# Routing from un-normed rows, a float32 gather of rows without scale and shift, and a second spare slot for weights

## The chip, the cores and the metric

The kernel runs on one core of a Trainium2 chip. The metric is the device time of one execution in microseconds (us). The profile is of one execution of its own; its times count from the start of its span.

## What is computed

Two layers of a decoder trunk over 256 tokens of width 2048, in float32. Each layer is a mixer (a state-space mixer in layer 0, sparse attention in layer 1) and a mixture of 32 experts with two normalisations around it:

```python
h = _layer_norm(DN_ALPHA * h + mix, ln_mix_g[i], ln_mix_b[i])
ffn = _hier_moe(h, moe_w_group[i], moe_b_group[i], moe_w_expert[i], moe_b_expert[i],
                moe_w_gate[i], moe_w_up[i], moe_w_down[i])
h = _layer_norm(DN_ALPHA * h + ffn, ln_ffn_g[i], ln_ffn_b[i])
```

`_layer_norm` is `(x - mean) * rsqrt(var + eps) * g + b` by rows. In `_hier_moe` each token takes one of 4 groups by `softmax(t @ w_group + b_group)` and two of that group's 8 experts by `t @ w_expert + b_expert`; an expert is `silu(t @ w_gate) * (t @ w_up)` of width 256, scaled by its gate and multiplied by `w_down`.

## The kernel before

The tokens lie on 128 partitions in two halves; `acc` holds the residual rows in float32 (128 x 2 x 2048).

**Weights.** All large weights come in tiles of 128 x 4096 float32 (2.10 MB), in the fixed order of `plan`. `issue()` starts the next load, `take()` hands out the next loaded tile. The tiles are in a ring of six buffers (`RING`), and during a mixture in one more, the spare, from the pool `one`: which entries of the plan use it is in the set `spare`, every seventh. SP issues all of them, in program order, and waits at each for its buffer's last readers. A mixture takes 8 tiles of gate and up weights and 4 of down weights for each four experts ("a round"; eight rounds, `qd` 0 to 7).

**Around the router.** `out_proj` ends a mixer: PE multiplies, VectorE adds into `acc` (L800) and takes row statistics. The last entry of the mixer's plan is `gb`, which fills a ring buffer with `ln_mix_g` and `ln_mix_b`, each broadcast to all partitions. In `moe`, `layer_norm` computes the reciprocal root by three Newton steps; VectorE's `centre` (L869) does `(acc - mean) * g` and `shift` (L873) `acc * rs + b`, both in place, eight of each with 512 strided columns. PE transposes the centred rows (L222), ScalarE copies them out to `xT`, and PE multiplies them by the router's 36 weight columns (L1048) in float32; `bw` and `sbw` bring in what the shift adds to the logits. VectorE then makes logits, maxima and masks (L1092 to L1111), PE counts positions by triangular products, and VectorE writes one-hot matrices `ohr` (L1168) of 128 slots, 32 for each of four experts.

**Gather and experts.** The gather (L64 under `gather`) brings the rows of the 128 slots together: PE multiplies the normed rows by the one-hot matrix. Rows are split into a rounded part `xr` (ScalarE, L1065) and a remainder `xl` (VectorE, `st_xl`, L1069), both fp32r, so a chunk of 128 columns takes four fp32r products. A gather has four quarters of four chunks, each copied to `xs` by ScalarE (L1185). `gate_up` (L1279) multiplies by half of a round's gate, then up weights, and calls `issue()` twice after each pair of tiles is used. Then SiLU and gate (L1202, L1204), transposes, and `st_down` with `w_down`: its four blocks each read all four down tiles. `scatter` brings the results back to `acc`. After round 1's `gate_up`, `past_cap` is a branch on the largest expert's token count (its body does not run in this trace).

## Time and profile before

| | us |
|---|---|
| Median of 3 runs | 1735.82 (1734.8 to 1739.2) |
| The profiled execution, its own time | 1736.97 |
| Its span | 1735.3 |

| Engine | busy us | share of the span |
|---|---|---|
| PE | 1495.7 | 86% |
| VectorE (DVE) | 760.8 | 44% |
| ScalarE (ACT) | 493.3 | 28% |
| GpSimd (POOL) | 100.7 | 6% |

The page gives the busy share of the 16 DMA engines and the bytes moved in 40 equal slices, 43.4 us each. The chain of waits follows the work that ended last backwards. The timeline lists an engine's instructions in order of time, merged; for SP these are DMA issues, and a long duration there is the time from the first issue of the group to the last. A table by windows gives each engine's busy time, PE's granted clock and the DMA's share in a stretch.

### The profile page before, as it was taken

The numbers are of one execution on the slowest core, as the hardware profiler recorded it, in microseconds if no ns is written. First come the engines' busy times: TensorE is split into PE (matmuls) and PEld (weight loads), VectorE is DVE, ScalarE is ACT, GpSimd is POOL, SyncE is SP. The second block draws the span as 40 slices with busy tenths as digits, with TensorE's granted clock in tenths as the row PEclk, the third lists the DMA queues.
The fourth block names the chain that finished last, engine by engine and source line by source line (L and its number), as shares of the span: only waits on it lengthen the run. The fifth ranks groups of instructions, "written<-read, shape, count | busy, mean of one in ns | idle before, by whom it ended". The sixth has DMA issues, their size and how long they took to land. (4 is left out here: it accounts for less than half of the span.)

```text
span 1735.3 us, 28757 instructions
## 1 busy us (share of the span) xinstructions
PE 1495.7 (86%) x12119; PEld 1053.0 (61%) x12119; DVE 760.8 (44%) x1636; ACT 493.3 (28%) x1040; POOL 100.7 (6%) x225
## 2 busy tenths in 40 slices
PE   8999999999977788677788999999986887777687
PEld 7888888988633444343347998988744343433343
DVE  5788897666422012112207677966720121122015
ACT  3455564543311001000013455544410011000011
POOL 2111100001000000000001001400200000000000
PEclk8999999999896788899889999999987898988988
DMA  9565223855699999999996644345599999999994
GB/s 293 181 139 98 95 99 128 284 195 226 254 418 382 425 422 415 424 412 417 418 417 243 249 145 153 131 146 194 188 417 424 382 419 424 418 401 412 424 419 190
DMA packets 112938, 517.18 MB, mean 298 GB/s; under 512 B 8368, under 2 KB 41376, under 8 KB 71072
## 3 DMA queue, kind: packets, MB, share of 16 engines
q1 hardware_dynamic: 109664, 507.93, 73.8%
q0 software_dynamic: 3136, 7.31, 2.4%
q8 instruction: 99, 1.62, 0.4%
q14 instruction: 39, 0.32, 0.1%
HBM read 509.97 MB, written 5.24 MB: 297 GB/s over the span
## 5 line engine op out<-in xcount | busy, mean ns | idle before, releaser
L1279 PE MATMUL gu<-ring,xs 128*32 128x256 f32 x4096 | 317.9, 433 | 108.8 <-DMA ring<-in_moe_w_up_dram 84.0
L1279 PEld LDWEIGHTS gu<-ring,xs 128*32 128x32 f32 x4096 | 149.4, 123 | 265.2 <-DMA ring<-in_moe_w_up_dram 108.6
L64 PE MATMUL yd<-ring,hT 128*32 128x512 f32 x1024 | 187.9, 749 | 59.5 <-DMA ring<-in_moe_w_down_dram 58.4
L1204 DVE SCALAR_TENSOR_TENSOR hh<-gu,gsl,sg 128x256 f32<-128x256 f32 x16 | 7.7, 484 | 436.4 <-ACT sg L1202 436.4
L80 DVE TENSOR_TENSOR spl<-ring,spr 128x512 fp32r<-128x512 f32 x176 | 122.3, 696 | 78.1 <-ACT spr L79 75.1
L64 PE MATMUL mm<-ohr,xr 128*128 128x128 f32 x512 | 128.1, 293 | 32.7 <-DVE ohr L1168 19.1
L64 PEld LDWEIGHTS yd<-ring,hT 128*32 128x32 f32 x1024 | 37.4, 129 | 177.4 <-DMA ring<-in_moe_w_down_dram 88.7
L79 ACT ACTIVATE spr<-ring 128x512 fp32r<-128x512 f32 x176 | 110.7, 631 | 110.3 <-DVE spl L80 51.3
L80 DVE TENSOR_TENSOR yl<-yd,yr 128x512 fp32r<-128x512 f32 x64 | 44.3, 692 | 211.4 <-ACT yr L79 211.4
L64 PEld LDWEIGHTS mm<-ohr,xr 128*128 128x128 f32 x512 | 106.0, 207 | 45.3 <-issue 41.6
L64 PE MATMUL mm<-ohr,xl 128*128 128x128 f32 x512 | 127.3, 291 | 0.0
L1185 ACT ACTIVATE xs<-mm 128x512 f32<-128x512 f32 x64 | 38.2, 597 | 303.4 <-PE mm L64 303.4
L64 PE MATMUL u<-xT,ring 128*128 128x256 f32 x512 | 122.1, 393 | 2.2 <-DMA ring<-in_s_w_in_dram 1.4
L79 ACT ACTIVATE yr<-yd 128x512 fp32r<-128x512 f32 x64 | 38.3, 599 | 263.7 <-PE yd L64 263.7
L64 PEld LDWEIGHTS u<-xT,ring 128*128 128x128 f32 x512 | 97.6, 196 | 17.3 <-DMA ring<-in_s_w_in_dram 1.8
L64 PEld LDWEIGHTS mm<-ohr,xl 128*128 128x128 f32 x512 | 106.4, 208 | 0.1
L1202 ACT ACTIVATE sg<-gu 128x256 f32<-128x256 f32 x16 | 6.1, 384 | 264.9 <-PE gu L1279 264.9
L1250 DVE TENSOR_TENSOR acc<-acc,ps 128x512 f32<-128x512 f32 x112 | 72.6, 681 | 10.0 <-PE ps L64 10.0
L64 PE MATMUL ps<-yr,sc 128*128 128x512 f32 x128 | 58.6, 458 | 3.0 <-DVE acc L1250 2.0
L64 PEld LDWEIGHTS ps<-yr,sc 128*128 128x128 f32 x128 | 23.9, 187 | 60.1 <-issue 55.9
L1270 DVE TENSOR_SCALAR sc<-mm,slotp 128x256 fp32r<-128x256 f32 x16 | 7.7, 484 | 103.0 <-PE mm L64 103.0
L64 PE MATMUL mm<-spr,q 128*128 128x512 f32 x128 | 51.2, 400 | 0.0
(411 smaller groups left out, 2617.2 us busy)
## 6 DMA issues: line engine op xcount, KB each, us to landing
ring<-in_moe_w_gate_dram SPq DMA_DIRECT2D x128, 1024.0 KB, 15.9
ring<-in_moe_w_up_dram SPq DMA_DIRECT2D x128, 1024.0 KB, 19.6
ring<-in_moe_w_down_dram SPq DMA_DIRECT2D x56, 2048.0 KB, 24.8
ring<-in_s_w_glu_dram SPq DMA_DIRECT2D x8, 2048.0 KB, 9.5
ring<-in_s_w_out_dram SPq DMA_DIRECT2D x8, 2048.0 KB, 12.6
ring<-in_moe_w_down_dram SPq DMA_DIRECT2D x16, 1024.0 KB, 20.0
ring<-in_dsa_w_out_dram SPq DMA_DIRECT2D x8, 2048.0 KB, 8.1
ring<-in_s_w_in_dram SPq DMA_DIRECT2D x7, 2048.0 KB, 13.7
```

Source lines behind the costliest of these rows:

```text
L64: T.matmul(o, l, r, start=start, stop=stop)
L79: S.activation(dst[0], src, AF.Copy)
L80: V.tensor_tensor(dst[1], src, dst[0].bitcast(F32), op=OP.subtract)
L1185: S.activation(xs[:, 4 * q:4 * q + 4], p.rearrange("p (a b) -> p a b", a=4), AF.Copy)
L1202: S.activation(sg, gu[:, 0:FF], AF.Silu)
L1204: V.scalar_tensor_tensor(hh, gu[:, FF:2 * FF], g, sg, op0=OP.mult, op1=OP.mult)
L1250: V.tensor_tensor(acc[:, h, bs], acc[:, h, bs], ps, op=OP.add)
L1270: V.tensor_scalar(scs[qd], p[:, 0:L], slotp, None, op0=OP.is_equal)
L1279: T.matmul(gu[es, k * FF:(k + 1) * FF], xss[qd][:, 8 * half + c, es], w[e // 2][:, e % 2, c, :], start=half + c + k == 0, stop=half == 1 a ...
```

## The change

- **Router.** PE transposes the un-normed `acc` rows. `wr` holds router weights times `ln_mix_g` in 64 columns (32 expert, 8 empty, 4 group, 20 empty), made by GpSimd; mean and shift enter afterwards, by column sums `sw` (one PE product) and per-row scalars. The logits' product has the weights stationary and 256 tokens moving, in two halves of PE's columns (`o` 0 and 64) that `sel` adds up.
- **Gather.** `xz` is `(acc - mean) * rs` in float32 (`st_z`: half 0 on VectorE, half 1 on ScalarE); `xr`, `xl` are gone. A chunk takes two float32 products instead of four fp32r ones. Scale and shift come on leaving PSUM, by chunk, from `gTc`: ScalarE, and in the first two quarters of round 0 VectorE for every other chunk.
- **Residual.** `acc` is left un-normed until `residual`, 16 VectorE instructions during the second `gate_up` of round 0, with `ln_mix_g` and `ln_mix_b` loaded broadcast into buffers of `xs`, `yr`, `yl`. `gb` is out of the plan.
- **Weights.** The spare has two buffers (`bufs=2`), so there are eight; `moe` calls `issue()` twice at its start, and once less after the norm.

```diff
@@ issue, plan_s5 (and plan_dsa alike)
-            t = (spare_pool[0] if i in spare else ringp).tile([P, 4096], F32, name="ring", tag="ring")
+            t = (spare_pool[0].tile([P, 4096], F32, name="ring", tag="ring", bufs=2) if i in spare else
+                 ringp.tile([P, 4096], F32, name="ring", tag="ring"))
-        plan.append(gb("ln_mix_g", "ln_mix_b", 0))
@@ plan_moe
-        i = RING - 1
-        while i < len(todo):
-            spare.add(len(plan) + i)
-            last_spare[li] = len(plan) + i
-            i += RING + (i + RING < at_gb)
+        last_spare[li] = []
+        for i in (RING, RING + 1):
+            while i < len(todo):
+                spare.add(len(plan) + i)
+                k = i
+                i += RING + 2 - (i > at_gb)
+            last_spare[li].append(len(plan) + k)
@@ moe
-            issue()
+            issue(); issue()
...
+            for i, n in enumerate(("ln_mix_g", "ln_mix_b")):
+                nc.sync.dma_start(gTc[:, i], dram(A[n], li * D, [[KC, P], [1, KC]]))
...
+            G.memset(wr, 0.0)
+            for i, t in ((0, wr), (1, wb)):
+                if i:
+                    G.memset(wb, 0.0)
+                for w, a, n in ((wex, 0, 32), (wge, 40, 4)):
+                    G.tensor_tensor(t[:, :, a:a + n], w, gbT[:, i, :, None].to_broadcast([P, KC, n]), op=OP.mult)
...
+            for i, t in ((0, wr), (1, wb)):
+                G.tensor_tensor(sw[:, :, i], t[:, 0:8, 0:44], t[:, 8:16, 0:44], op=OP.add)
+            for n in (4, 2, 1):
+                G.tensor_tensor(sw[:, 0:n], sw[:, 0:n], sw[:, n:2 * n], op=OP.add)
...
-            centre, shift, rs = layer_norm(stt)
...
-            for q in range(4):
-                st_h(q)
-            issue()
+            def logits(b):
+                for c in range(4 * b, 4 * b + 4):
+                    o = 64 * (c % 2)
+                    T.matmul(plT[o:o + 64, 0:L], wr[:, c, :], xT[b][:, c % 4, :], start=c < 2, stop=c >= KC - 2,
+                             skip_group_check=True)
+            mv, ve = ln_moments(stt)
+            for b in range(NBLK):
+                for c in range(0, 4, 2):
+                    p = pmm.tile([P, 512], F32, name="mm")
+                    for c2 in range(2):
+                        for h in range(2):
+                            T.transpose(p[:, c2 * 256 + h * 128:c2 * 256 + (h + 1) * 128],
+                                        acc[:, h, b * CB + c + c2:(b + 1) * CB:4], ident)
+                    S.activation(xT[b][:, c:c + 2, :], p.rearrange("p (a b) -> p a b", a=2), AF.Copy)
+                if b:
+                    logits(b - 1)
+            mm(junk[:, 0:88], ones.to_broadcast([P, P]), sw[:, 0].rearrange("p i n -> p (i n)"), True, True)
...
+            logits(NBLK - 1)
+            def st_z(q, h):
...
+                if h:
+                    S.activation(o, i, AF.Identity, scale=rs[:, h:h + 1], bias=nr[:, h:h + 1])
+                else:
+                    V.tensor_scalar(o, i, mv[:, h, 0:1], rs[:, h:h + 1], op0=OP.subtract, op1=OP.mult)
...
+            S.activation(plS, plT[:, 0:L], AF.Copy)
+            for h in range(2):
+                mm(pl[:, h, 0:56], plS[:, h * 128:(h + 1) * 128], sel, True, True)
+            keep_warm(plT, 12)
...
+                V.scalar_tensor_tensor(lg[:, h], gs56, nm[:, h:h + 1], pl[:, h, 0:56], op0=OP.mult, op1=OP.add)
+                V.scalar_tensor_tensor(lg[:, h], lg[:, h], rs[:, h:h + 1], rbias, op0=OP.mult, op1=OP.add)
...
@@ gather
-                        for src in (xr, xl):
-                            mm(p[:, c * P:(c + 1) * P], src[:, h, (4 * q + c) * P:(4 * q + c + 1) * P],
-                               ohr[:, h].rearrange("p a b -> p (a b)"), i == 0, i == 3)
-                S.activation(xs[:, 4 * q:4 * q + 4], p.rearrange("p (a b) -> p a b", a=4), AF.Copy)
+                        mm(p[:, c * P:(c + 1) * P], xz[:, h, (4 * q + c) * P:(4 * q + c + 1) * P],
+                           ohr[:, h].rearrange("p a b -> p (a b)").bitcast(F32), h == 0, h == 1)
+                for c in range(4):
+                    k = 4 * q + c
+                    g, b = gTc[:, 0, k:k + 1], gTc[:, 1, k:k + 1]
+                    if first and c % 2:
+                        V.tensor_scalar(xs[:, k], p[:, c * P:(c + 1) * P], g, b, op0=OP.mult, op1=OP.add)
+                    else:
+                        S.activation(xs[:, k], p[:, c * P:(c + 1) * P], AF.Identity, scale=g, bias=b)
@@ residual (new), and its calls in round 0
+            def residual(k):
+                c = slice(k % 4 * CB, (k % 4 + 1) * CB)
+                for h in range(2):
+                    if k < 4:
+                        V.scalar_tensor_tensor(acc[:, h, c], acc[:, h, c], mv[:, h, 0:1], mixg[:, c], op0=OP.subtract, op1=OP.mult)
+                    else:
+                        V.scalar_tensor_tensor(acc[:, h, c], acc[:, h, c], rs[:, h:h + 1], mixb[k % 4], op0=OP.mult, op1=OP.add)
...
+            mixg = xs_tile().rearrange("p c n -> p (c n)")
+            nc.sync.dma_start(mixg, dram(A["ln_mix_g"], li * D, [[0, P], [1, D]]))
+            mixb = [wk.tile([P, CB], F32, name=n, tag=n) for n in ("yr", "yl") for _ in range(2)]
+            for b in range(NBLK):
+                nc.sync.dma_start(mixb[b], dram(A["ln_mix_b"], li * D + b * CB, [[0, P], [1, CB]]))
-            st_xl(2); st_xl(3)
...
-                    gate_up(0, 1)
+                    gate_up(0, 1, lambda c: residual(c - 8))
```

How rows move on three engines, around the router of layer 0 (lines of the changed kernel differ from those of the kernel before).

SP's queue, before, from the last weights of the mixer's projection on (`x4` is two tiles of gate or up weights, or four of down weights):

```order
L137 DMA ring<-in_s_w_out_dram 128x8x512 x8
L143 DMA ring<-in_ln_mix_g_dram 128x2048
L144 DMA ring<-in_ln_mix_b_dram 128x2048
L933 DMA ring<-in_moe_w_gate_dram 128x2048 x4
L933 DMA ring<-in_moe_w_up_dram 128x2048 x4
L933 DMA ring<-in_moe_w_gate_dram 128x2048 x4
L933 DMA ring<-in_moe_w_up_dram 128x2048 x4
L949 DMA ring<-in_moe_w_down_dram 128x4096 x4
```

and in the changed kernel:

```order
L138 DMA ring<-in_s_w_out_dram 128x8x512 x8
L928 DMA ring<-in_moe_w_gate_dram 128x2048 x4
L928 DMA ring<-in_moe_w_up_dram 128x2048 x4
L928 DMA ring<-in_moe_w_gate_dram 128x2048 x4
L928 DMA ring<-in_moe_w_up_dram 128x2048 x4
L992 DMA gTc<-in_ln_mix_g_dram 128x16
L992 DMA gTc<-in_ln_mix_b_dram 128x16
L1416 DMA xs<-in_ln_mix_g_dram 128x2048
L1419 DMA yr<-in_ln_mix_b_dram 128x512 x2
L1419 DMA yl<-in_ln_mix_b_dram 128x512 x2
L944 DMA ring<-in_moe_w_down_dram 128x4096 x4
```

The two megabyte-sized broadcast loads moved from ahead of round 0's weights to behind all eight of its gate and up tiles.

VectorE, before, from the last Newton step to the masks' end and the one-hot matrices:

```order
L869 SCALAR_TENSOR_TENSOR acc<-acc,ln_mv,ring 128x128x4 x4
L1080 TENSOR_REDUCE sbw<-junk 128x36
L1081 TENSOR_TENSOR rbias<-rbias,sbw 128x36
L873 SCALAR_TENSOR_TENSOR acc<-acc,rs_y,ring 128x128x4 x8
L1092 SCALAR_TENSOR_TENSOR gl<-pl,rs_y,rbias 128x4 x2
...
L1111 TENSOR_TENSOR am<-er,el 128x64
L1069 TENSOR_TENSOR xl<-acc,xr 128x512 x2
L1122 SCALAR_TENSOR_TENSOR pos<-mm,am 128x64
```

and in the changed kernel, from the same place on, and then round 0's slot gates, the residual and the SiLU product `hh`:

```order
L1100 TENSOR_SCALAR xz<-acc,ln_mv,rs_y 128x512 x2
L1086 COPY gs_4417<-junk 128x44
L1087 TENSOR_TENSOR rbias<-rbias,junk 128x44
L1116 SCALAR_TENSOR_TENSOR lg<-gs_4417,nm,pl 128x56 x2
...
L1135 TENSOR_TENSOR am<-er,lg 128x64
L1145 SCALAR_TENSOR_TENSOR pos<-mm,am 128x64
...
L1223 COPY gsl<-mm 32x1 x4
L1246 SCALAR_TENSOR_TENSOR acc<-acc,ln_mv,xs 128x512 x8
L1248 SCALAR_TENSOR_TENSOR acc<-acc,rs_y,yr 128x512 x4
L1248 SCALAR_TENSOR_TENSOR acc<-acc,rs_y,yl 128x512 x4
L1230 SCALAR_TENSOR_TENSOR hh<-gu,gsl,sg 128x256
```

Of these rows, twelve passes over a quarter of a half's columns left the stretch before the logits, two left the stretch before `pos`, and sixteen passes now stand between round 0's slot gates and its `hh`.

PE, in the changed kernel, from the last product of the projection to the first `gate_up`:

```order
L64 MATMUL mm<-spl,sTr 128x512
L1077 MATMUL mm<-ident,acc 128x128 x16
L1066 MATMUL junk<-xTa,wr 64x256 x4
L1077 MATMUL mm<-ident,acc 128x128 x8
L1066 MATMUL junk<-xTb,wr 64x256 x4
L1077 MATMUL mm<-ident,acc 128x128 x8
L1066 MATMUL junk<-xTa,wr 64x256 x4
L64 MATMUL junk<-sw,ones 128x88
L1066 MATMUL junk<-xTb,wr 64x256 x4
L64 MATMUL pl<-sel,plS 128x56 x2
...
L64 MATMUL mm<-ohr,xz 128x128 x16
L1314 MATMUL gu<-ring,xs 32x256 x64
```

The logits are 16 products of 256 columns where 32 of 36 stood, and a product with `sw` now stands ahead of the last four of them.

## Rows read from the trace of the kernel before

**Rows 1.** The page: busy share of the DMA engines in tenths, and GB/s, in 40 slices of 43.4 us.

```profile
DMA  9565223855699999999996644345599999999994
GB/s 293 181 139 98 95 99 128 284 195 226 254 418 382 425 422 415 424 412 417 418 417 243 249 145 153 131 146 194 188 417 424 382 419 424 418 401 412 424 419 190
```

**Rows 2.** The chain of work that ended last, in order of time, one round of layer 1: start, us, what.

```profile
1419.50 16.10 DMA ring<-in_moe_w_gate_dram
...
1435.65 4.94 PE gu L1279 x55
...
1440.61 24.73 DMA ring<-in_moe_w_down_dram
...
1465.38 6.01 PE yd L64 x26
...
1480.12 16.10 DMA ring<-in_moe_w_gate_dram
```

**Rows 3.** SP's timeline (DMA issues): start, us from the first to the last issue of the group, and what is loaded, around both routers and at round 1 of layer 0.

```profile
419.63 2.05 SPq L933 DMA_DIRECT2D ring<-in_moe_w_gate_dram  x4
438.77 17.49 SPq L933 DMA_DIRECT2D ring<-in_moe_w_up_dram  x4
456.36 12.59 SPq L949 DMA_DIRECT2D ring<-in_moe_w_down_dram  x4
...
529.87 30.15 SPq L933 DMA_DIRECT2D ring<-in_moe_w_up_dram  x4
560.12 2.00 SPq L933 DMA_DIRECT2D ring<-in_moe_w_gate_dram  x4
...
1236.72 17.02 SPq L933 DMA_DIRECT2D ring<-in_moe_w_up_dram  x4
```

**Rows 4.** Windows of 2 us, layer 0: busy time (and instructions) of PE, PEld, DVE, ACT, POOL, then PE's granted clock, the DMA engines' share, GB/s.

```profile
446.00:448.00 2.00, 2.00 (x13) 1.95 (x11) 1.97 (x4) 0.60 (x1) 0.00 (x0) 0.56 0.03 12
454.00:456.00 2.00, 2.00 (x44) 1.11 (x40) 1.08 (x6) 0.62 (x2) 0.00 (x0) 1.00 0.22 41
...
554.00:556.00 2.00, 2.00 (x18) 0.57 (x11) 1.37 (x3) 0.23 (x1) 0.00 (x0) 1.00 0.92 381
556.00:558.00 2.00, 2.00 (x16) 0.78 (x18) 1.60 (x3) 0.37 (x1) 0.00 (x0) 1.00 0.22 90
558.00:560.00 2.00, 2.00 (x16) 0.83 (x12) 0.81 (x2) 0.60 (x1) 0.00 (x0) 1.00 0.29 45
560.00:562.00 2.00, 1.93 (x26) 0.71 (x18) 1.71 (x4) 0.00 (x0) 0.00 (x0) 1.00 0.80 295
```

**Rows 5.** VectorE's timeline, layer 0's router; the last row is of layer 1.

```profile
422.55 0.69 DVE L800 SCALAR_TENSOR_TENSOR acc<-acc,mm 128x512 f32<-128x512 f32 x1 [0.62 <-PE mm L64]
...
424.99 0.75 DVE L869 SCALAR_TENSOR_TENSOR acc<-acc,ln_mv,ring 128x512 f32<-128x512 f32 x1
...
430.11 2.73 DVE L869 SCALAR_TENSOR_TENSOR acc<-acc,ln_mv,ring 128x512 f32<-128x512 f32 x4
...
433.36 5.38 DVE L873 SCALAR_TENSOR_TENSOR acc<-acc,rs_y,ring 128x512 f32<-128x512 f32 x8
438.67 0.34 DVE L1092 SCALAR_TENSOR_TENSOR gl<-pl,rs_y,rbias 128x4 f32<-128x4 f32 x2
...
441.46 0.22 DVE L1111 TENSOR_TENSOR am<-er,el 128x64 f32<-128x64 f32 x1
441.62 1.95 DVE L1069 TENSOR_TENSOR xl<-acc,xr 128x512 fp32r<-128x512 f32 x2
...
443.73 0.49 DVE L1168 TENSOR_TENSOR ohr<-slot,pos 128x128 fp32r<-128x128 f32 x2
...
1261.40 0.66 DVE L1197 COPY gsl<-mm 32x1 f32<-32x1 f32 x4 [0.58 <-PE mm L64]
```

**Rows 6.** PE's and ScalarE's timelines, layer 0 (the row at 1246.81 is of layer 1). A float32 product of PE shows as two records: the one at 437.76 is 16 products of the program, x32; a float32 transpose and an fp32r product show as one.

```profile
428.73 0.68 PE L222 MATMUL mm<-ident,acc 128*128 128x128 f32 x4
435.99 1.93 PE L1048 MATMUL pl<-wr,xT 128*128 128x36 f32 x16
436.69 7.84 ACT L1065 ACTIVATE xr<-acc 128x512 fp32r<-128x512 f32 x8
437.76 3.82 PE L64 MATMUL junk<-ident 128*128 128x128 f32 x32
444.17 0.30 PE L64 MATMUL mm<-ohr,xr 128*128 128x128 f32 x1 [1.72 <-DVE ohr L1168]
446.20 0.37 PE L64 MATMUL mm<-ohr,xr 128*128 128x128 f32 x1
449.40 8.89 PE L1279 MATMUL gu<-ring,xs 128*32 128x256 f32 x128
513.25 3.65 PE L1279 MATMUL gu<-ring,xs 128*32 128x256 f32 x60 [1.85 <-DMA ring<-in_moe_w_gate_dram]
546.23 6.50 PE L64 MATMUL yd<-ring,hT 128*32 128x512 f32 x32
...
1246.81 9.54 PE L1279 MATMUL gu<-ring,xs 128*32 128x256 f32 x128
```

**Rows 7.** GpSimd's timeline, layer 0's router.

```profile
419.63 1.16 POOL L1010 TENSOR_TENSOR bw<-wr,bT 128x576 f32<-128x576 f32 x1 [77.85 <-ACT wr L1006]
428.71 1.26 POOL L1034 TENSOR_TENSOR gbl<-gb,gbr 8x512 fp32r<-8x512 f32 x1
```

More of the change, by code (lines that the diff above doesn't have):

```diff
@@ L1000, in moe @@
[L1000 to L1002 removed]
+            gTc = sm("gTc", [P, 2, KC])
+            for i, n in enumerate(("ln_mix_g", "ln_mix_b")):
+                nc.sync.dma_start(gTc[:, i], dram(A[n], li * D, [[KC, P], [1, KC]]))
+            xT = [prp.tile([P, 4, L], F32, name="xTa")]
+            plS = prp.tile([P, L], F32, name="plS")
+            wr = prp.tile([P, KC, 64], F32, name="wr")
@@ new lines, in moe @@
+            wex = prp.tile([P, KC, NEXP], F32, name="wex")
+            wge = prp.tile([P, KC, 4], F32, name="wge")
+            gbT = prp.tile([P, 2, KC], F32, name="gbT")
+            wb = prp.tile([P, KC, 44], F32, name="wb")
+            xT.append(prp.tile([P, 4, L], F32, name="xTb"))
+            xT += xT
+            gb8 = prp.tile([8, 2, 256], F32, name="gb8")
+            for i, n in enumerate(("ln_mix_g", "ln_mix_b")):
+                G.dma_start(gbT[:, i], dram(A[n], li * D, [[4, P], [CB, NBLK], [1, 4]]))
@@ L1034, in moe @@
             G.tensor_tensor(gbl, gb8, gbr.bitcast(F32), op=OP.subtract)
-            sbw = prp.tile([P, 36], F32, name="sbw")
-            xT += [prp.tile([P, 4, L], F32, name=f"xT{i}") for i in range(1, 4)]
-            xr = one.tile([P, 2, D], F32R, name="xr")
-            xl = one.tile([P, 2, D], F32R, name="xl")
+            xz = one.tile([P, 2, D], F32, name="xz")
             pl = plg.tile([P, 2, 256], F32, name="pl")
             pjk = pool(pre, "mjk", 2, side="right", **PS)
-            junk, pbw = (pjk.tile([P, 512], F32, name="junk") for _ in range(2))
@@ L1043, in moe @@
-            cut = lambda t, q: t.rearrange("p (k c) -> p k c", c=KC)[:, :, 4 * q:4 * q + 4]
-            def logits(c0):
-                for c in range(c0, c0 + 2):
-                    for h in range(2):
-                        T.matmul(pl[:, h, 0:36], xT[c // 4][:, c % 4, h * 128:(h + 1) * 128], wr[:, c, :], start=c + h == 0,
-                                 stop=c == KC - 1, skip_group_check=True)
-            for k in range(2):
-                mm(pbw[:, 0:288], ones.to_broadcast([P, P]), bw[:, 8 * k:8 * k + 8].rearrange("p c n -> p (c n)"), k == 0, k == 1)
@@ L1054, in moe @@
-            keep_warm(pmm.tile([P, 512], F32, name="mm"), 8)
-            centre, shift, rs = layer_norm(stt)
-            xcut = lambda t, h, q: t[:, h].rearrange("p (c k) -> p c k", c=KC)[:, 4 * q:4 * q + 4]
-            ccut = lambda t, h, q: t[:, h].rearrange("p (k c) -> p c k", c=KC)[:, 4 * q:4 * q + 4]
-            def st_h(q):
-                for h in range(2):
-                    shift(q, h)
-                for h in range(2):
-                    S.activation(xcut(xr, h, q), ccut(acc, h, q), AF.Copy)
@@ L1067, in st_xl @@
-            def st_xl(q):
-                for h in range(2):
-                    V.tensor_tensor(xcut(xl, h, q), ccut(acc, h, q), xcut(xr, h, q).bitcast(F32), op=OP.subtract)
-            for q in range(4):
-                if q > 1:
-                    for h in range(2):
-                        centre(q, h)
-                for c in range(4 * q, 4 * q + 4, 2):
-                    transpose_x(acc, xT[q], pmm, (c,), 4 * q)
-                    keep_warm(junk, 0)
-                    if c:
-                        logits(c - 2)
@@ L1080, in moe @@
-            V.tensor_reduce(sbw, pbw[:, 0:288].rearrange("p (c n) -> p n c", c=8), axis=AX.X, op=OP.add)
-            V.tensor_tensor(rbias, rbias, sbw, op=OP.add)
-            logits(KC - 2)
-            keep_warm(junk, 16)
-            for q in range(4):
-                st_h(q)
-            issue()
+            junk, plT = (pjk.tile([P, 512], F32, name="junk") for _ in range(2))
+            def logits(b):
[3 more added lines that the diff above has]
+                             skip_group_check=True)
```

75 lines of the change are left out of this document (38 added, 37 removed).

## The prediction

> **What bounds the kernel now.** I read the 40 slices of the page first [rows 1]. In two stretches, slices 11 to 20 and 29 to 38, the DMA engines are busy throughout at 380 to 425 GB/s: these are the mixtures, 870 us of the span. Elsewhere the DMA is half idle, and in slice 10 (254 GB/s) it is partly idle too: there the router runs. The chain of waits says the same of a round [rows 2]: PE works a few us between a DMA wait of 16 us and one of 25 us, and a round takes 1480.12 - 1419.50 = 60.6 us for twelve tiles, so **one tile costs 5.05 us** of DMA time (2.10 MB at 415 GB/s). So inside a mixture PE, VectorE and ScalarE are hidden; the mixture ends when its 96 tiles have landed, plus a fixed tail. Only two things move its end: when the DMA, stopped by full buffers, may start again, and how many tiles it has by then.
>
> SP's timeline shows the stops [rows 3]. Two tiles go out from 419.63; the next (two issues, one tile) only at 438.77, where `shift` has read the last of `gb`; then nothing until the group's last issues at 438.77 + 17.49 = 456.26, where the first `gate_up` gives buffers back. The windows show the DMA at 12 GB/s at 446 and 41 at 454 [rows 4]. Layer 1 repeats it (1236.72, 17.02 us) [rows 3]. A second stop is in round 1: SP is held from 529.87 until 560.12 [rows 3], and four windows are short of 420 GB/s by 39, 330, 375 and 125, times 2 us: 1.7 MB, or 4.1 us [rows 4].
>
> **Part 1, router to first `gate_up`.** Now VectorE adds the last projection block from 422.55 [rows 5] and `gate_up` begins at 449.40 [rows 6]: 26.9 us. The changed order, from 422.5:
> - PE needs no centred rows, so the 2.4 us until the first `centre` at 424.99, and its passes [rows 5], drop out of the way. 32 transposes at 0.125 us [rows 6] are 4.0 us. The logits are 16 products of 256 columns, 32 records, two column halves side by side; by `gate_up`'s pace of 0.243 us for a set of side-by-side records (60 records, four abreast, in 3.65) [rows 6], 16 x 0.243 = 3.9 us. Now they are 64 records of 0.12 [rows 6], 7.7 us. With `sw`'s product (0.25) and half a microsecond for the first copies, PE is done at about 431.1.
> - The copy `plS` and two small products: 1.0 us; four combining VectorE instructions, 0.8 us as the rows from 438.67 take for the same step, and the masks to 441.68, 2.4 us more [rows 5]: 435.3.
> - Between masks and one-hot matrices `xl` takes 1.95 us now [rows 5]. Without it PE's small products set the pace, some 0.7 us by estimate, then `pos` and `ohr`, 0.7 us: the gather begins at 436.7 instead of 444.17 [rows 6], **7.5 us earlier**.
> - Gather: 16 float32 products are 32 records. A float32 128 x 128 record takes 3.82 / 32 = 0.12 us [rows 6], so two quarters take 3.8 us; now 32 fp32r records take 444.17 to 449.40, 5.2 us, since the granted clock falls to its lower level on the way (0.56 at 446) [rows 4]. The product count halves, PE's work does not. At 2.4 GHz throughout the gather gains 1.4 us, at 1.2 GHz it loses 2.5.
>
> `gate_up` thus begins 8.9 us earlier at best and 5 us at worst; I take 8.5, nearest the row in which the clock stays up, since PE now idles less before the gather: the idle 1.72 us [rows 6] shrinks to that 0.7 plus 0.7.
>
> The Trainium skill ("TensorE: Matmul & The Clock Gate", Part 1) says that the lower rate is the default and activity lifts it. The trace agrees in kind: the fall follows the idle stretch. By it alone the up-clock case would hold here, a gain of 8.9.
>
> GpSimd's chain for `sw` begins at the last projection product, and PE needs it some 7.5 us later. By `bw`'s 1.16 us for 576 columns [rows 7], 2.0 ns each, the 1,896 columns of products and sums after that point take 3.8 us, and clears and two load issues 2 us by estimate: 5.8 us, 1.7 less than it has (`wr` itself waits for nothing late). `gbl` (512 columns) took 1.26 beside VectorE's passes [rows 7], 2.5 ns each; at that pace 6.7 us, still hidden.
>
> The Trainium skill ("GPSIMD Engine Reference", Key points) says that GpSimd shares its SBUF interfaces with VectorE and contends with two-input instructions. The slower `gbl` row agrees. At twice `bw`'s pace 9.6 us would be needed, PE would wait 2.1 us per layer, and the time would be 1710; rival 4 is the far end of this.
>
> **Part 2, one more tile by then.** `gb`'s ring buffer goes to a weight tile, and the spare is doubled: when the first `gate_up` hands back its buffers, eight tiles are in, not seven. That is one tile fewer to come: **-5.05 us**. They fit: three tiles from 419.63 land by about 435, the hand-back comes at about 441 + 4. The 2 MB of broadcast loads are not saved, they move: SP issues them when the small products have run, about 432, behind the tiles, done by 440, inside the idle stretch that is 10 us long now [rows 4]. If that cover were gone they would cost 5 us, at the head of the down tiles' queue. So 0, with 5 as the other end.
>
> **Part 3, the stop in round 1.** An eighth buffer holds 5.05 us of DMA work; the stop is 4.1. The gather after the branch is 0.9 us slower at the lower clock (32 records, 0.24 for 0.21 us). Take **-3.2 us**, between 0 and -4.1.
>
> **Part 4, the residual.** Sixteen VectorE passes at 5.38 / 8 = 0.67 us [rows 5] stand before round 0's `hh`: 10.8 us. They begin when the slot gates are read; in layer 1 these end at 1262.06 [rows 5], 5.7 us after the first `gate_up` (1246.81 + 9.54) [rows 6]. With `gate_up` at 440.9 and 7.8 us long (32 x 0.243), they run from 454.4 to 465.2, while PE is done at about 461; so `hh`, the next gather (3.8, or 7.7 at 1.2 GHz) and `st_down` are late by 4 us against now. Queued behind `hh` are `ohr` of round 1 and all of `st_down`, whose buffers SP waits for. `st_down` of about 12 us (13.7 in round 1, from 546.23 [rows 6] to the issue at 560.12 [rows 3]) then ends at 483 to 488. From 445 the DMA has eight tiles it may load, 40 us: until 485. So the loss is 0 to 4 us, 7 if both clock effects fall badly; I take **+1.5**. The same passes left the router, where part 1 counts them; ScalarE's `xr` (7.84) [rows 6] is replaced by four passes that run beside PE. The gather's exits (four scaled copies for one) are hidden inside rounds by the DMA waits.
>
> **Sum.** -8.5 - 5.05 - 3.2 + 1.5 = -15.2 us per layer, -30.5 us for two. The profiled execution took 1736.97: 1706.5; the median of the runs is 1.2 below it: **1706 us**. Ends per layer: -8.9, -5.05, -4.1, 0 = -18; and -5, -5.05, 0, +4 = -6, and 5 less if the broadcast loads are not covered.
>
> **Rivals.**
> 1. Better: the hand-back comes earlier by more than `gate_up`'s start. It took 6.9 us of 449.40 to 456.26 at a partly lower clock; at 0.243 it takes 3.9. If PE stays at 2.4 GHz, 1.5 to 2 us more per layer, and the round-1 stop vanishes: -20 per layer, 1696. For it: less idle. Against: the first `gate_up` fell to the lower clock in both layers (8.89 and 9.54 us for 7.8) [rows 6].
> 2. The residual starves the DMA in round 0: 7 us lost, gather at 1.2 GHz: -5 - 5.05 - 3.2 + 7 = -6 per layer, 1724. For it: `hh` is late by 10.8 us of passes. Against: 40 us of tiles in hand.
> 3. The second spare does nothing: its buffer lies where the projection's operands lie and SP waits. Then part 2 and 3 go: -7 per layer, 1722. Against: only the last product of the projection need pass, 20 us before the hand-back.
> 4. Slower: `sw`. Its product stands in PE's queue ahead of the last logits; the routing, gather and hand-back wait for it, one for one. It decides from 7.5 us after the last projection product; to be slower than before it must take 15 us longer than that, 23 us, four times my 5.8. At 25 us both layers lose 2 to 3 us: 1741. Against: no GpSimd row is near that pace.
>
> **How the numbers follow.** Forecast 0.60 (1698 to 1714); rival 1 0.16, rival 2 0.12, rival 3 0.05, rival 4 with its lighter forms 0.07, half of these within 0.3% of before (about what a measurement tells from no change: 5.2 us). Range: 1692 to 1724, from a little beyond rival 1 to rival 2; it leaves out rival 4 and parts of 1 and 3. Faster 0.92, same 0.04, slower 0.04.
>
> **What would show it.** `gate_up` 18 to 19 us after the last projection block, not 26.9; eight tiles issued before the first hand-back, and the broadcast loads landed by then; rounds still 60 us; no trough after the branch in round 1; a DMA trough near the end of round 0 sizes part 4. A `gate_up` that begins as late as now, a wait of PE on GpSimd, or a trough in round 0 longer than 7 us would make the prediction wrong.

## Result and the profile after

The changed kernel takes 1694.37 us (median of 4 runs, 1693.63 to 1695.37); the kernel before, beside it, 1737.51. The ratio is 0.9737, 95% interval 0.9708 to 0.9765: 2.6% faster. The forecast was 1706: it had the direction and four of the places, and was 12 us too high. (0.9737 of the 1735.82 that the prediction started from is 1690, just under its range.) The profiled execution took 1694.67 us, its span is 1692.7: 42.6 less than before.

The page, DMA share in tenths and GB/s in 40 slices, now of 42.3 us, beside [rows 1]:

```profile
DMA  9665322955999999999996634344799999999994
GB/s 289 197 139 96 105 101 66 326 194 186 362 409 422 424 423 421 424 424 421 424 415 279 256 120 179 107 153 187 292 420 423 424 420 425 423 422 422 424 417 162
```

The slice of layer 0's router has 362 GB/s where it had 254, and the slices of the mixtures no longer dip to 382 or 401: nearly all stand at 420 to 425. So a full DMA moves about 422 GB/s here, and the 415 that I read from a round of before had stops in it.

SP's timeline (start, us from the group's first to its last issue, what is loaded), as in [rows 3]; the last row is of layer 1:

```profile
420.60 3.06 SPq L928 DMA_DIRECT2D ring<-in_moe_w_up_dram  x4
...
433.21 0.33 SPq L1416 DMA_DIRECT2D xs<-in_ln_mix_g_dram  x1
...
434.73 2.22 SPq L1419 DMA_DIRECT2D yl<-in_ln_mix_b_dram  x2
446.07 4.26 SPq L944 DMA_DIRECT2D ring<-in_moe_w_down_dram  x4
...
517.03 13.79 SPq L928 DMA_DIRECT2D ring<-in_moe_w_up_dram  x4
542.76 1.76 SPq L928 DMA_DIRECT2D ring<-in_moe_w_gate_dram  x4
...
1221.55 4.27 SPq L944 DMA_DIRECT2D ring<-in_moe_w_down_dram  x4
```

Eight tiles are out before the hand-back at 446.07 (the first issue after the first `gate_up` has read its tiles). Before, it was at 454.88, in layer 1 at 1252.94; the prediction took 456.26, which is the end of the second issue in the merged row of [rows 3]. In a narrower window of the kernel before that row is

```profile
454.88 1.38 SPq L933 DMA_DIRECT2D ring<-in_moe_w_up_dram  x2
```

Counted from the router's last statistics (423.88 and 1221.77 before, 424.01 and 1199.80 now), the hand-back comes at 22.1 and 21.8 us instead of 31.0 and 31.2: 8.9 and 9.4 us earlier. The broadcast loads go out at 433 to 437; in round 1 SP has its buffers back at 542.76, 25.7 us after 517.03, where it needed 30.2.

PE's timeline, as in [rows 6], the last row of layer 1:

```profile
437.66 0.46 PE L64 MATMUL mm<-ohr,xz 128*128 128x128 f32 x2 [0.35 <-DVE ohr L1191]
438.84 3.62 PE L64 MATMUL mm<-ohr,xz 128*128 128x128 f32 x30 [0.72 <-DVE ohr L1191]
442.38 7.11 PE L1314 MATMUL gu<-ring,xs 128*32 128x256 f32 x128
...
466.96 3.33 PE L64 MATMUL mm<-ohr,xz 128*128 128x128 f32 x14 [5.24 <-DVE ohr L1191]
...
1217.86 7.11 PE L1314 MATMUL gu<-ring,xs 128*32 128x256 f32 x128
```

The first `gate_up` starts 7.0 us earlier (forecast 8.5) and now takes 7.11 us in both layers, not 8.89 and 9.54. So the hand-back follows 3.7 us behind its start in both layers, not 5.5 and 6.1. At 466.96 PE has waited 5.24 us for the one-hot matrix of round 1, which stands behind the residual and `hh` on VectorE.

VectorE's timeline, layer 0, as in [rows 5]:

```profile
425.94 2.36 DVE L841 SCALAR_TENSOR_TENSOR rs_y<-rs_t,rs_y 128x2 f32<-128x2 f32 x1
...
433.04 0.20 DVE L1087 TENSOR_TENSOR rbias<-rbias,junk 128x44 f32<-128x44 f32 x1 [1.39 <-DMA rbias<-in_moe_b_group_dram]
...
437.22 1.56 DVE L1191 TENSOR_TENSOR ohr<-slot,pos 128x128 fp32r<-128x128 f32 x2
...
455.41 5.39 DVE L1246 SCALAR_TENSOR_TENSOR acc<-acc,ln_mv,xs 128x512 f32<-128x512 f32 x8
```

Three things that I had not counted: an instruction on two elements a partition takes 2.36 us, a wait for a small load, and one-hot passes of 1.56 us where they took 0.49 [rows 5].

**Where the 42 us came from.** In a mixture the weights set the pace, so I ask for how long the DMA had nothing to load. I take windows of 1 us from 3 us ahead of the router's last statistics to `sg` (the SiLU) of each round, sum 1 - (GB/s)/422 over them, and call it the shortfall. The fifth column is another measure, without a rate: by how much the weight tiles landed earlier, counted from the same statistics, over the first twelve tiles, the next twelve, the twelve after them, and up to the last gate and up tile.

| us, layer 0 / layer 1 | shortfall before | after | gained | tiles landed earlier | forecast |
|---|---|---|---|---|---|
| router, to `sg` of round 0 | 20.4 / 20.3 | 6.5 / 6.1 | 13.9 / 14.1 | 13.7 / 13.9 | 13.55 (parts 1, 2) |
| end of round 0 (residual) | 0.2 / 0.6 | 1.2 / 0.1 | -1.0 / 0.5 | -1.1 / 0.8 | -1.5 (part 4) |
| round 1 | 3.9 / 4.2 | 0.1 / -0.1 | 3.8 / 4.2 | 4.7 / 3.4 | 3.2 (part 3) |
| rounds 2 to 7 | 2.6 / 3.9 | -0.1 / 0.1 | 2.8 / 3.8 | 1.7 / 2.3 | 0 |
| sum | 27.1 / 28.9 | 7.6 / 6.2 | 19.5 / 22.6 | 18.9 / 20.5 | 15.2 |

From the statistics to the last `sg` layer 0 takes 449.7 us instead of 468.6, layer 1 451.4 instead of 471.8: 39.4 less, as the landings say. The shortfall's 42.1 is 2.7 more than that; so its cells are good to a microsecond or so, and that it nearly equals the 42.6 of the span is chance. (The two kernels' shortfalls can be compared because they move about the same bytes in these windows: the changed one has one weight tile fewer to load, and the broadcast loads instead.) The missing 3.2 us lie between the layers, where neither the forecast nor the shortfall looks. At the end of layer 0, GpSimd and VectorE, before and then now:

```profile
918.96 5.33 POOL L1488 TENSOR_TENSOR spl<-ring,spr 128x1168 fp32r<-128x1168 f32 x2
920.62 3.70 DVE L859 TENSOR_SCALAR ln_ve<-ln_mv 128x2 f32<-128x2 f32 x1
```

```profile
897.15 5.38 POOL L1527 TENSOR_TENSOR spl<-ring,spr 128x1168 fp32r<-128x1168 f32 x2
901.83 0.77 DVE L854 TENSOR_SCALAR ln_ve<-ln_mv 128x2 f32<-128x2 f32 x1
```

VectorE's instruction on two elements ends with GpSimd's two passes in both, and the last normalisation waits for it: 2.9 us. GpSimd reaches these passes 3 us earlier, counted from the last `sg`, in the changed kernel; why it does, no run here shows.

The last line but one of the table is a term that the forecast lacks. Four windows of the kernel before, rounds 4 and 5 of layer 1 (columns as in [rows 4]), and SP's row show it:

```profile
1538.00:1540.00 2.00, 2.00 (x20) 1.09 (x20) 0.95 (x2) 0.60 (x1) 0.00 (x0) 1.00 0.77 213
1540.00:1542.00 2.00, 1.93 (x19) 0.75 (x12) 1.62 (x3) 0.00 (x0) 0.00 (x0) 1.00 0.89 356
1542.00:1544.00 2.00, 2.00 (x34) 1.04 (x36) 0.69 (x1) 0.00 (x0) 0.00 (x0) 1.00 0.87 295
...
1600.00:1602.00 2.00, 2.00 (x20) 0.98 (x20) 1.27 (x3) 0.60 (x1) 0.00 (x0) 1.00 0.66 197
```

```profile
1512.82 27.19 SPq L933 DMA_DIRECT2D ring<-in_moe_w_up_dram  x4
```

PE works with hardly a pause there and the DMA is short: SP stands at its up tiles until `st_down` gives buffers back at 1540. Of the changed kernel's 2 us windows from round 1 to the last `sg` none is under 393 GB/s. The chain of [rows 2] had the sign of it: between its rows at 1465.38 and 1480.12 it runs through PE's scatter and SP's issue,

```profile
1477.37 1.15 PE ps L64 x4
1478.52 0.14 SPq L933
```

so that round's next load, too, had waited for `st_down`.

### The profile page after: what moved, and what is told of

The parts are those of the page before. It is cut to its first block, busy times and chain, and to the rows that moved or that the text cites. A ratio compares the mean times of both kernels' runs of the same rounds, so it can differ in the third digit from the quotient of the medians.

```text
span 1692.7 us, 28774 instructions
## 1 busy us (share of the span) xinstructions
PE 1458.1 (86%) x12011; PEld 1027.2 (61%) x12011; DVE 759.5 (45%) x1640; ACT 541.1 (32%) x1214; POOL 118.1 (7%) x249
## 3 DMA queue, kind: packets, MB, share of 16 engines
HBM read 510.02 MB, written 5.24 MB: 304 GB/s over the span
## 5 line engine op out<-in xcount | busy, mean ns | idle before, releaser
L1314 PE MATMUL gu<-ring,xs 128*32 128x256 f32 x4096 | 304.1, 422 | 98.0 <-DMA ring<-in_moe_w_up_dram 80.2
L1314 PEld LDWEIGHTS gu<-ring,xs 128*32 128x32 f32 x4096 | 145.0, 120 | 245.5 <-DMA ring<-in_moe_w_up_dram 105.7
L64 PE MATMUL yd<-ring,hT 128*32 128x512 f32 x1024 | 181.0, 719 | 47.3 <-DMA ring<-in_moe_w_down_dram 46.3
L1211 ACT ACTIVATE xs<-mm,gTc 128x128 f32<-128x128 f32 x248 | 93.9, 456 | 282.9 <-PE mm L64 280.9
L64 PE MATMUL mm<-ohr,xz 128*128 128x128 f32 x1024 | 131.5, 290 | 38.0 <-DVE ohr L1191 24.6
L64 PEld LDWEIGHTS mm<-ohr,xz 128*128 128x128 f32 x1024 | 125.4, 203 | 51.2 <-issue 33.0
L64 PE MATMUL ps<-yl,sc 128*128 128x512 f32 x128 | 50.5, 395 | 0.0
L64 PE MATMUL mm<-spl,q 128*128 128x512 f32 x128 | 50.5, 395 | 0.0
## 6 DMA issues: line engine op xcount, KB each, us to landing
ring<-in_s_w_out_dram SPq DMA_DIRECT2D x8, 2048.0 KB, 12.1
ring<-in_s_w_in_dram SPq DMA_DIRECT2D x7, 2048.0 KB, 13.6
```

What stands on the lines that cost most here:

```text
L64: T.matmul(o, l, r, start=start, stop=stop)
L1211: S.activation(xs[:, k], p[:, c * P:(c + 1) * P], AF.Identity, scale=g, bias=b)
L1314: T.matmul(gu[es, k * FF:(k + 1) * FF], xss[qd][:, 8 * half + c, es], w[e // 2][:, e % 2, c, :], start=half + c + k == 0, stop=half == 1 a ...
```

## Experiments

Each is an edit of the changed kernel, compared with its 1694.37. Beside the small edits it ran again, as `after_again`:

> The changed kernel once more, on the same chip and in the same rounds as the three small edits: 1694 (1693 to 1696).

Measured 1693.08 (1689.45 to 1695.59): differences under 3 us between groups of runs say little.

### What the eighth buffer is worth

`one_spare`:

```diff
-            t = (spare_pool[0].tile([P, 4096], F32, name="ring", tag="ring", bufs=2) if i in spare else
+            t = (spare_pool[0].tile([P, 4096], F32, name="ring", tag="ring", bufs=1) if i in spare else
...
-        for i in (RING, RING + 1):
+        for i in (RING,):
...
-                i += RING + 2 - (i > at_gb)
+                i += RING + 1 - (i > at_gb)
...
-            issue(); issue()
+            issue()
```

> The changed kernel with one spare slot in place of two, all else kept. Theory A (what the two traces' windows say: the eighth buffer is worth its own tile, the stop of round 1 and the short dips of the later rounds): 5 us for the tile, 4 for the stop, 2.5 to 3.5 for the dips, per layer, so +12 to +13 per layer: 1694.4 + 25 = 1719 (1715 to 1723), and dips under 340 GB/s again in round 1 and in two or three of the rounds 4 to 6. Theory B (as predicted: the tile and the round-1 stop alone, 5.05 + 3.2): 1711 (1708 to 1713). Theory C (a buffer is worth only its tile): 1704.5.

Measured 1708.83 (1708.18 to 1712.95), +14.5. Shortfall: router 11.1 / 10.8, round 1 0.1 / 0.0, rounds 2 to 7 5.3 / 2.9. The tile and the later stops came back (by landings the tiles of rounds 2 to 7 take 4.7 us longer in both layers together, and the first twelve 4.1 in each). **The stop of round 1 did not**, which neither A nor B allows; that B's time was met is chance. SP's timeline of this kernel in round 1:

```profile
520.26 25.23 SPq L928 DMA_DIRECT2D ring<-in_moe_w_up_dram  x4
545.60 1.94 SPq L928 DMA_DIRECT2D ring<-in_moe_w_gate_dram  x4
```

SP waits 25.2 us, not the 30.15 of before [rows 3], with seven tiles at most, as before. So PE gave the buffers back sooner, and I looked at its clock.

### The clock behind the branch

`pairs1` (one spare) and `pairs2` (two) go back to four fp32r products a chunk in the gathers of rounds 1 to 7, where `pair` is true; `xz` becomes an fp32r tile, so the low parts are left out, and two of each four products are overwritten:

```diff
-            xz = one.tile([P, 2, D], F32, name="xz")
+            xz = one.tile([P, 2, D], F32R, name="xz")
...
+                    if pair:
+                        for h, a, z in ((0, True, True), (1, True, True), (0, True, False), (1, False, True)):
+                            mm(p[:, c * P:(c + 1) * P], xz[:, h, (4 * q + c) * P:(4 * q + c + 1) * P],
+                               ohr[:, h].rearrange("p a b -> p (a b)"), a, z)
+                        continue
```

> one_spare, and the gathers of rounds 1 to 7 as 64 fp32r records each, as before the change, in place of 32 float32 records (the low parts are left out and two of each four products are thrown away, so that only the kind and number of records is as before). Theory A (the stop of round 1 went because the granted clock comes back during a float32 gather and did not during an fp32r one): the gather behind the branch takes 7 us and the first yd group 6.5 again, SP's group behind it ends about 30 us after sg, DMA short by 3 to 4 us in round 1, 1708.8 + 6 to 9 = 1715 to 1718. Theory B (the stop depended on the buffers, as predicted, and is gone in one_spare for another reason than the gather): as one_spare, 1708 to 1710.

> The same edit of the gathers with both spare slots kept. Theory A: the gather behind the branch and the first yd group are as slow as in pairs1, but the eighth buffer (5 us of DMA work) covers a stop of 4: DMA short by 0 to 1 us in round 1, 1694 to 1697. Theory B: 1694 to 1695, and no slower PE either. If the eighth buffer covers nothing there: 1701 to 1703.

(The text miscounts: two quarters are 32 records in either form, a round 64.) Measured:

| us | fp32r pairs in rounds 1 to 7 | float32 |
|---|---|---|
| one spare | 1720.35 (1717.24 to 1725.14) | 1708.83 |
| two spares | 1697.07 (1694.10 to 1700.18) | 1694.37 |

Theory A holds, with both times a little above its ranges. In `pairs1` the shortfall of round 1 is 5.4 / 4.1, in `pairs2` 0.1 / 0.0. PE of `pairs1`, then SP:

```profile
532.40 7.06 PE L64 MATMUL mm<-ohr,xz 128*128 128x128 f32 x32 [7.38 <-PEq L1365]
...
541.33 6.21 PE L64 MATMUL yd<-ring,hT 128*32 128x512 f32 x32
```

```profile
524.05 30.27 SPq L928 DMA_DIRECT2D ring<-in_moe_w_up_dram  x4
```

The same two rows of PE in the changed kernel:

```profile
525.83 5.96 PE L64 MATMUL mm<-ohr,xz 128*128 128x128 f32 x32 [6.94 <-PEq L1360]
...
533.14 3.64 PE L64 MATMUL yd<-ring,hT 128*32 128x512 f32 x32
```

And the granted clock (the third number from the right), of the changed kernel and then of `pairs2`:

```profile
528.00:530.00 2.00, 2.00 (x11) 2.00 (x11) 0.00 (x0) 0.31 (x1) 0.00 (x0) 0.50 0.96 393
530.00:532.00 2.00, 2.00 (x19) 1.70 (x17) 0.00 (x0) 1.36 (x5) 0.00 (x0) 0.91 1.03 430
```

```profile
532.00:534.00 2.00, 2.00 (x11) 2.00 (x11) 0.00 (x0) 0.53 (x2) 0.00 (x0) 0.50 1.03 430
...
538.00:540.00 2.00, 2.00 (x16) 0.50 (x12) 0.00 (x0) 0.04 (x1) 0.00 (x0) 0.50 0.97 401
540.00:542.00 2.00, 2.00 (x17) 0.35 (x9) 0.69 (x1) 0.56 (x1) 0.00 (x0) 0.83 1.01 422
```

PE idles 7 us at the branch and both kernels start the gather at 1.2 GHz. With float32 records the clock is back at 2.4 GHz some 4.5 us into the gather; with fp32r records, as many and PE as busy during the gather, it is not back until the down products, about 13 us after the gather's start. Layer 1 repeats it: the gather behind the branch takes 5.47 us in the changed kernel and 7.06 in `pairs1`. The stop of round 1 thus had two remedies in this change, and either suffices: the float32 gather or the eighth buffer. All that each does, in every round, comes to -11.5 us for the float32 gather with one spare, and to -23.3 us for the buffer with pairs, -14.5 without. On top of the buffer the gather's 2.7 us are within the scatter of the runs; its gain in round 0 (`pairs2` is 3.0 / 3.1 short there, after 1.2 / 0.1) is of the profiles alone.

### Does the end follow the hand-back

`delay`:

```diff
-            keep_warm(plT, 12)
+            keep_warm(plT, 37)
```

> 25 more junk products (50 records, 6.04 us at 2.90/24 us a record) behind the pl products, so that the masks' count products wait for PE: the first hand-back should come about 5.3 us later in both layers. Theory A (the end follows the first hand-back one for one): +10.6, 1705 (1703 to 1707). Theory B (three tiles and the broadcast loads are still landing until 443.7, so part of a delay is absorbed): +4 or less, under 1699.

Measured 1702.10 (1700.56 to 1705.87), +7.7, between the two theories' times. But the hand-back is 449.30 - 423.46 = 25.8 us behind the router's statistics, where it was 446.07 - 424.01 = 22.1, and 4.0 later in layer 1, together 7.7: the delay was smaller than planned, since PE had 0.7 us to spare and the one-hot passes no longer met GpSimd's work. One for one, as A says.

### Are the broadcast loads hidden

`bcast_more`:

```diff
+            for _ in range(3):
-            nc.sync.dma_start(mixg, dram(A["ln_mix_g"], li * D, [[0, P], [1, D]]))
+                nc.sync.dma_start(mixg, dram(A["ln_mix_g"], li * D, [[0, P], [1, D]]))
```

> The 1 MB broadcast load of the gain is made three times, 2.1 MB more per layer, 4.95 us of DMA time at 423 GB/s. Theory A (the loads hide in the idle stretch ahead of the first hand-back, which is now 3.7 us long in layer 0 and 2.9 in layer 1): +1.2 and +2.0, together +3, 1697.5 (1696 to 1699); the windows show no idle stretch ahead of the hand-back any more. Theory B (the loads were never hidden, they stand at the head of the down tiles' queue): +10, 1704. Theory C (the loads cost nothing whatever their size): 1694.4.

Measured 1710.57, +16, beyond every theory, and the run doesn't answer the question: SP stood from 433.36 to 448.74 at the three loads into one tile, as if each waited for the one before it, and the down tiles behind them on SP's queue went out only at 450.97, 26.8 us behind the statistics. `bcast_none` asks it without that:

```diff
-            nc.sync.dma_start(mixg, dram(A["ln_mix_g"], li * D, [[0, P], [1, D]]))
+            G.memset(mixg, 1.0)
```

(and alike for `mixb`, with 0.0; the kernel then leaves out this gain and shift in the residual).

> The 2 MB of broadcast loads are left out, constants set by GpSimd stand in their tiles (so the residual is computed with gain 1 and shift 0). Theory A (they lie in a stretch in which the DMA has nothing else it may load): the idle stretch ahead of the hand-back grows by about 5 us to 8 and the end does not move, 1693 to 1695. Theory B (they take DMA time from the tiles): 1694.4 - 10 = 1684.5.

Measured 1694.96 (1691.65 to 1699.81): no gain, theory A. Its windows:

```profile
436.00:438.00 2.00, 2.00 (x13) 2.00 (x13) 2.00 (x2) 0.00 (x0) 2.00 (x5) 0.59 0.01 4
...
442.00:444.00 2.00, 2.00 (x45) 1.18 (x38) 1.17 (x10) 1.97 (x7) 0.00 (x0) 1.00 0.00 0
444.00:446.00 2.00, 2.00 (x44) 1.23 (x40) 1.32 (x8) 0.95 (x2) 0.00 (x0) 1.00 0.81 213
```

The DMA idles some 9 us ahead of this hand-back, and the 2 MB that it did not move bought nothing: theory B's 10 us are excluded. A gain of up to 2 us isn't, since the hand-back comes 1.6 and 0.5 us later behind the statistics than in the changed kernel (in layer 0 the gather runs at the lower clock, 0.59 in the window at 436). The router's shortfall is 12.9 / 11.7 here with the time unchanged, so shortfalls of two kernels can be compared only where they move the same bytes.

### The clock ahead of the first `gate_up`

`no_junk`:

```diff
-            keep_warm(plT, 12)
+            keep_warm(plT, 0)
```

> The 12 junk products behind the pl products are left out, so PE is idle from about 433 to 436.5 but for nothing. Theory A (an idle stretch ahead of the gather lets the granted clock fall, as before the change, where it was 0.56 in the window at 446): the gather takes 5 to 7.7 instead of 4.3 us and the first gate_up 8.9 or more instead of 7.11; first hand-back 3 to 5 us later per layer, 1700 to 1704. Theory B (the clock is held by the transposes and products before, not by the junk): granted clock 1.00 up to 454, time 1694 to 1695.

Measured 1698.88 (1697.14 to 1701.88), +4.5. Theory A holds for the gather only. PE's rows, layer 0:

```profile
434.75 0.21 PE L64 MATMUL mm<-ab,oneb 128*1 128x32 bf16 x2 [3.59 <-DVE ab L1134]
...
436.70 5.16 PE L64 MATMUL mm<-ohr,xz 128*128 128x128 f32 x32 [0.91 <-DVE ohr L1191]
441.79 7.11 PE L1314 MATMUL gu<-ring,xs 128*32 128x256 f32 x128
```

After 3.59 us of idle the gather takes 5.16 (6.26 for 30 records in layer 1), but the clock is back, during the float32 gather, before `gate_up`, which takes 7.11 again. Router shortfall: 7.9 / 9.1 for 6.5 / 6.1, again one for one.

### The residual

`resid_double` puts an idle pass of equal size ahead of each of the 16:

```diff
+                    V.scalar_tensor_tensor(acc[:, h, c], acc[:, h, c], 1.0, acc[:, h, c], op0=OP.mult, op1=OP.max)
```

> Ahead of each of the 16 residual passes a pass of the same size that leaves the value as it is: hh of round 0 is 10.7 us later. Theory A (in round 0 the DMA runs out of free buffers about when st_down gives them back: short by 1.1 us in layer 0, 0.1 in layer 1): +9 to +10 in layer 0 and +6 to +10 in layer 1, 1694.4 + 15 to 20 = 1709 to 1714. Theory B (tiles in hand cover it): under 1698.

Measured 1716.03 (1714.62 to 1719.07), +21.7: all of the 21.4 us of added passes. Theory A, 2 us above its range, and no slack at all; windows of layer 0:

```profile
485.00:490.00 5.00, 4.82 (x42) 1.94 (x42) 1.79 (x6) 1.30 (x4) 0.00 (x0) 1.00 0.23 97
490.00:495.00 5.00, 5.00 (x39) 1.79 (x38) 3.57 (x6) 0.90 (x2) 0.00 (x0) 1.00 0.01 3
```

The tiles in hand last until 486, as the prediction had worked out (485). `resid_early` takes the passes out of the way:

```diff
             st_gates()
+            for k in range(8):
+                residual(k)
...
-                    gate_up(0, 1, lambda c: residual(c - 8))
+                    gate_up(0, 1)
```

> The 16 residual passes follow st_gates directly, in VectorE's idle time during the first gate_up, and no longer stand between the slot gates and hh of round 0. PE's idle 5.2 us ahead of round 1's gather should go in both layers. Theory A (the DMA was short by 1.1 us in round 0 of layer 0 and by 0.1 in layer 1, and only that can come back): -1, 1693 to 1694. Theory B (the residual costs the 1.5 us per layer of the prediction): -3, 1691.4. Theory C (passes of the early place hold up sc and gsl of round 0 and with them gate_up): 1695 or more.

Measured 1693.63 (1690.38 to 1695.44): PE's idle ahead of round 1 shrinks from 5.24 to 1.40 us, the shortfall there from 1.2 / 0.1 to nothing, and no gain that the runs can show. That is A's size. The residual costs what it stands over the edge, one for one, and in the changed kernel it stands just at it.

### The router's small waits

`path` loads `rbias` ahead of `wr`, and lets VectorE make `gbr` and `gbl` behind `st_gates`:

```diff
-            gb8 = prp.tile([8, 2, 256], F32, name="gb8")
+            gb8 = one.tile([8, 2, 256], F32, name="gb8")
...
+            rbias = prp.tile([P, 56], F32, name="rbias")
+            G.memset(rbias, PAD)
+            G.dma_start(rbias[:, 0:32], dram(A["moe_b_expert"], li * 32, [[0, P], [1, 32]]))
+            G.dma_start(rbias[:, 40:44], dram(A["moe_b_group"], li * 4, [[0, P], [1, 4]]))
             G.memset(wr, 0.0)
...
-            G.tensor_copy(gbr, gb8)
-            G.tensor_tensor(gbl, gb8, gbr.bitcast(F32), op=OP.subtract)
...
                 V.tensor_tensor(g4[:, :, 1], gt, g4[:, :, 0].bitcast(F32), op=OP.subtract)
+                V.tensor_copy(gbr, gb8)
+                V.tensor_tensor(gbl, gb8, gbr.bitcast(F32), op=OP.subtract)
```

> rbias is loaded ahead of GpSimd's products with the gains, and gbr and gbl are made by VectorE behind st_gates, not by GpSimd beside the one-hot passes. Theory A (the one-hot passes take 1.56 and 1.24 us instead of 0.49 because GpSimd works beside them; the rbias wait costs nothing as the pl product ends at the same moment): gather complete 0.7 to 1.2 us earlier in both layers, 1692 to 1693. Theory B (the 1.39 us wait for rbias in layer 0 also counts): 1690.5 to 1691.5. Theory C (the one-hot passes are slow for another reason): 1694 to 1695.

Measured 1712.53 (1710.23 to 1715.46), +18, which no theory had. GpSimd's timeline has the router's first load, in the changed kernel and then in `path`; the third fence is PE's timeline in `path`:

```profile
337.11 0.77 POOL L1004 DMA_DIRECT2D gbT<-in_ln_mix_g_dram  x1 [119.18 <-DVE sTl L720]
```

```profile
420.51 0.77 POOL L1004 DMA_DIRECT2D gbT<-in_ln_mix_g_dram  x1 [203.41 <-DVE acc L794]
```

```profile
431.36 1.98 PE L1064 MATMUL junk<-xTa,wr 128*64 128x256 f32 x8 [7.16 <-POOL wr L1019]
```

The load into the router's first tile now waits for VectorE's additions of the projection (`acc`, L794) and comes 83 us later, and PE waits 7.16 us for `wr`. I take it that without `gb8` the router's tiles lie a little elsewhere, the first of them over a buffer of the projection; `path_fix` below undoes the move of `rbias` and the gap of `gb8` at once, so which of the two did it isn't separated. `sw` is ready at 437.6, some 16 us behind the last projection product, but PE reaches its product only at 438.3: the wait that counts is the one for `wr`, of which the prediction said that it waits for nothing late. The router's shortfall is 13.6 / 14.5, 7.1 / 8.4 more: a wait of PE on GpSimd ahead of the logits costs one for one, as rival 4 says, though by another tile than its `sw`. `comb` (`path` with `resid_early`) repeats it:

> Both edits together. If they add: 1691 to 1692.5, faster than either kernel.

Measured 1712.59 (1712.06 to 1713.69). `path_fix` leaves `rbias` where it was and keeps a tile of `gb8`'s size, set and never read, among the router's:

```diff
+            pad = prp.tile([8, 2, 256], F32, name="pad")
```

> path without its first edit, and with an unused tile of gb8's size kept among the router's tiles, so that these keep their places: gb8 loaded to another tile, gbr and gbl made by VectorE behind st_gates. Theory A (the one-hot passes are slow because GpSimd makes gbr and gbl beside them, and the first hand-back counts one for one): one-hot passes 0.49 us together, gather complete 0.7 to 1.2 us earlier in both layers, DMA short by about 1 us less in each, 1691 to 1692.5. Theory B (GpSimd's two instructions cost nothing): 1693 to 1694.5. If the router's first loads still come late: 1710 and more, as path.

Measured 1691.72 (1690.90 to 1693.45), 0.9720 of before (0.9700 to 0.9741). Its rows of VectorE and PE:

```profile
436.28 0.49 DVE L1193 TENSOR_TENSOR ohr<-slot,pos 128x128 fp32r<-128x128 f32 x2
```

```profile
436.72 3.81 PE L64 MATMUL mm<-ohr,xz 128*128 128x128 f32 x32 [0.35 <-DVE ohr L1193]
440.46 7.11 PE L1316 MATMUL gu<-ring,xs 128*32 128x256 f32 x128
```

Theory A: the one-hot passes are back at 0.49, `gate_up` begins 17.4 us behind the statistics instead of 18.4. The gain, 1.4 to 2.7 us against the two groups of runs of the changed kernel, is about what they scatter: in the later profile of the unchanged kernel (`after_again`) these passes took 0.55 and 0.79 us with GpSimd's two instructions beside them all the same. `path_fix_resid` adds `resid_early`:

> path_fix and resid_early together: 1690.5 to 1692 if path_fix gains 2 us and the residual's place up to 1; faster than either kernel, but by little more than the runs scatter.

Measured 1691.71 (1690.49 to 1692.99), 0.9722 of before (0.9702 to 0.9743): with `path_fix` the best of the study, by little more than the scatter.

## Why the forecast was right in kind and too small

- **What bounds the kernel**: right. The end followed the hand-back and the tiles in hand one for one (`delay`, `no_junk`, `resid_double`). But "one tile costs 5.05 us" was read from a round that contained stops; at 422 GB/s it is 4.97.
- **Part 1**: -8.5 was forecast for `gate_up`'s start, -7.0 came. The 1.5 are the one-hot passes beside GpSimd (1.0, `path_fix`) and waits ahead of them. The hand-back gained more than the start did, 8.9 and 9.4, because `gate_up` ran at 2.4 GHz: that is **rival 1** (1696, chance 0.16), with PE at 2.4 GHz and no stop in round 1. My argument against it, that the first `gate_up` fell to the lower clock in both layers, did not hold behind the float32 gather; that the old gather's form was the reason is shown behind the branch (`pairs1`), not here. Rival 1's 6.9 us from start to hand-back were a misreading, 5.5 in layer 0.
- **GpSimd's chain**: 7.9 us by the trace (422.47 to 430.40) where I estimated 5.8. It is hidden, but with nothing to spare in layer 0, where PE's product with `sw` starts at 430.45.
- **Part 2**: right. With part 1 13.55 was forecast; 13.9 and 14.1 came by shortfall, 13.7 and 13.9 by landings. That the sum fits so well is partly luck: a start that came later than forecast and a hand-back that followed it sooner nearly cancel. The broadcast loads are hidden to within 2 us (`bcast_none`).
- **Part 3**: 3.2 forecast, 3.8 and 4.2 measured, and its reason was half wrong: I priced the float32 gather at the lower clock 0.9 us *slower*; it is faster there (5.96 for 7.06), because the clock comes back during it, and it removes the stop without the buffer.
- **The step that failed**: everything outside the four parts was put at nothing, as "a fixed tail" and "rounds still 60 us". I had looked for stops in round 1 alone. Rounds 2 to 7 held 2.6 and 3.9 us of them, and the eighth buffer removes these too (`one_spare` has them, and in part `pairs1`; `pairs2` has not). In time that is 3.9 us for both layers by the landings, 0.3 a round, so a round still looks like 60 us. The end of layer 0 wasn't fixed either: 3.2 us, from one VectorE instruction of 3.70 us that takes 0.77. Of the 12.1 us by which the sum of 30.5 falls short of the span's 42.6, these two make 7.1. The residual makes 2.8 (+1.5 per layer forecast, 0.2 for both layers measured), part 3 1.6, parts 1 and 2 0.5. The kernel before has one profile, so a term of a microsecond or two rests on one trace of it.
- **Part 4**: right mechanism, and its edge (485) was right to a microsecond. PE came to the next gather in time, as the clock returned quickly once more; so the loss stayed near the lower end of 0 to 4, and +1.5 was too much. (`st_down` of round 1 is 13.9 us, not 13.7.)
- **Rivals 2 to 4**: none came. `resid_double` shows rival 2's mechanism and `path` a wait of PE on GpSimd akin to rival 4's, which bite one for one as soon as their slack is used up; `one_spare` excludes 3.
